# Last pair of output tiles of a two-layer streaming encoder by seven products, with the final norm in two halves of 320 tokens

## The chip, the cores and the metric

The kernel runs on one core of one Trainium2 chip. The metric is device time in microseconds (us) of one execution; lower is better. Engines are named as in the profile: PE (TensorE, matmuls) and PEld (its weight loads), DVE (VectorE), ACT (ScalarE), POOL (GpSimd) and SP (SyncE, which here only issues transfers). L12 is line 12 of the kernel before.

## What is computed

Two layers of a streaming encoder on 640 tokens (512 of a prompt, 8 x 16 of samples) with 2048 features. Each layer normalises its input, projects it with `w_in`, runs a convolution group, a window attention and a memory attention, and ends with one output projection and a residual. A last RMS norm follows the second layer:

```python
def rms_norm(x, g):
    y = x * rsqrt(mean(x * x, axis=-1, keepdims=True) + EPS)
    return y * g
...
y = concatenate([y_a, y_b, y_c], axis=-1) @ w_out      # (640, 2048) @ (2048, 2048)
x = x + y                                              # end of each layer
...
y_prompt, y_sample = rms_norm(hp, final_norm_g), rms_norm(hs, final_norm_g)
```

The mean of the last norm goes over all 2048 features of a token, so no token can be normalised before all its features are there.

## The kernel before, in words

Activations lie transposed: features on the 128 partitions, tokens along the free axis. `R` holds 16 row tiles (k = 0 to 15) of 128 features x 640 tokens in fp32. For a product each operand is split in a rounded part and a rest (`split`, L137: ACT rounds, L138, DVE subtracts, L139), and three matmuls (high x high, high x low, low x high) stand for one fp32 product. `HL` holds both parts of the 16 input tiles; `TA` and `TB` are tokens 0 to 319 and 320 to 639.

The output projection makes row tile j from 16 input tiles. Tiles 0 and 1 are done directly (`proj`, PE line L760). Tiles 2 to 15 are done in pairs (j1, j2) by `s_pair`: on 12 of the 16 input tiles (`KA`, `KB`) a 2 x 2 block scheme of Strassen's kind takes seven products of 18 matmuls for eight, on sums and differences of the weights (`sr`, made by DVE, L789 and L843) and of the inputs (`T[1]` to `T[4]`, tiles `th`, `tl`); the other four input tiles (`KS`, `rest`) are multiplied directly. All matmuls of `s_pair` are on L821 (`s_mm`): those into PSUM tiles `a` are the products on combined inputs (`mixed`) and the first product, those into `z` are `plain` and `rest`. A pair is 174 matmuls of 320 columns. The split weights (`sh`, `sl`) have two buffers each, so a split waits until PE has used up the one before the last. `add_to` (L827) adds each product to `R` on DVE. After a pair, `add_sq` squares each finished tile on ACT (L254, into `w`) and adds it into `acc` on DVE (L255).

`combos` builds `T` once per layer while PE works on tile 1: DVE subtracts in `R` in place (L789), then ACT and DVE split the differences.

In layer 1 the loop ends after tile 13; the last two tiles (14, 15) are multiplied directly (L1145, tokens 0 to 383 first, then 384 to 639). They need the upper half of inputs `KA`, which `combos` overwrites: it is saved to `y12d` in DRAM ahead of `combos` by a POOL transfer and read back in `turn`, which also replaces the buffers of `T` by buffers for the eight weight tiles (`xr`, `xh`, `xl`); for that the pair (12, 13) runs in another order (`early`: products on `T` first).

The norm: squares are summed over partitions by fp32 matmuls with a vector of ones (`tok_cols`, L222), `rsqrt` (L187 to L198) takes 12 small DVE steps, `tok_rows` (L212) spreads the result along tokens by fp32 matmuls with the identity. Then DVE multiplies each row tile by the feature factor and the row in one operation (L1178), and SP and ACT store two row tiles at a time (L1183). This is done for tokens 0 to 383 while the other tokens are multiplied, and after that for these.

All engines run their queue in order. The order in each queue is set when the program is built, by a planner that sees priorities (`tc.high_priority`) and explicit bounds (`tc.issue_after`).

Of the kernel before, what the change touches and what calls it, by code (L numbers as in the profile page):

```python
# [9 lines left out]
F32 = mybir.dt.float32  # L10
# [6 lines left out]
P = 128  # L17
D = 2048
# [40 lines left out]
def build(nc, tc, ctx, A):  # L59
# [69 lines left out]
    y12d = dr.tile([P, 6, HT], F32, tag="y12d", name="y12d")  # L129
# [87 lines left out]

    def tok_cols(srcs, inv, n=5):
        psc = pa()
        for t in range(n):  # L220
            for i, a in enumerate(srcs):
                m = pe.matmul(  # L222
                    psc[:, t:t + 1], a[:, t * P:(t + 1) * P], ones, start=i == 0, stop=i == len(srcs) - 1
                )
        cols = sml([P, n])
        col_rstd(cols, psc, n, inv)
        return cols, m.ins
# [678 lines left out]
    for l in range(L):  # L906
# [166 lines left out]
        if l == L - 1:  # L1073
            gp.dma_start(y12d, R[:, KA, TB])
# [3 lines left out]
        T, W = None, []  # L1078

        def t_prep(src):  # L1080
            with tc.high_priority():
                raw = tl([P, 512], "xr", 2, F32, cur["tw"])
                load(raw, src)
                hi = tl([P, 512], "xh", 8, F32R, cur["tw"])
                lo = tl([P, 512], "xl", 8, F32R, cur["tw"])
                split(raw, None, hi, lo)
                return hi, lo

        def turn(step):
            if step == 0:  # L1090
                close_pool("tt")
                open_pool("tw" if l == L - 1 else "wp", "right")
            if l < L - 1:
                return
            if step == 0:
                cur["y12"] = tl([P, 6, HT], "y12", 1, F32, cur["tw"])
                with tc.high_priority():
                    gp.dma_start(cur["y12"], y12d)
                return
            for p in (range(2), range(2, 8))[step - 1]:  # L1100
                W.append(t_prep(A["w_out"][l, NK - 2 + p // 4][:, p % 4 * 512:(p % 4 + 1) * 512]))
            if step == 1:
                b12 = hl(KA, TB)
                for g in (0, 3):
                    ks = slice(g, g + 3)
                    split(cur["y12"][:, ks, :], None, b12[0][:, ks, :], b12[1][:, ks, :])

        for j in list(range(2)) + list(range(2, done, 2)):
# [7 lines left out]
            else:  # L1116
                s_pair(l, j, T, resid, turn if j + 2 == done else None)
# [14 lines left out]
    ntok = [cs.stop - cs.start for cs in parts]
    sums, cols, rows, at = [None] * 2, [None] * 2, [None] * 2, []

    def in_order(f, *a):
        with tc.issue_after(at[0]) if at else nullcontext():
            r, m = f(*a)
        at[:] = [m]
        return r

    def products(ps, cs, j, k):
        wh, wl = W[j * 4 + k // 4]
        ws = slice(k % 4 * P, (k % 4 + 1) * P)
        for n, (w, lo) in enumerate(((wh, 0), (wh, 1), (wl, 0))):
            m = pe.matmul(  # L1145
                ps, w[:, ws], HL[:, lo * NK + k, cs], start=k == 0 and n == 0, stop=k == NK - 1 and n == 2
            )
        return None, m.ins

    def col_step(i):  # L1150
        cols[i] = in_order(tok_cols, [acc[:, parts[i]], sums[i]], 1.0 / D, ntok[i] // P)

    def row_step(i):
        rows[i] = in_order(tok_rows, cols[i], ntok[i] // P)[0][:, :ntok[i]]

    for i, cs in enumerate(parts):
        for j in range(2):
            ps = pz()[:, 0, :ntok[i]]
            for k in range(NK):
                if i == 1 and j == 0 and k == 5:  # L1160
                    col_step(0)
                if i == 1 and j == 0 and k == 14:
                    row_step(0)
                in_order(products, ps, cs, j, k)
            o = R[:, NK - 2 + j, cs]
            evac = ve.tensor_tensor(out=o, in0=ps, in1=res[j][:, cs], op=ALU.add)
            if j == 0:
                evac0 = evac
            sums[i] = w25()[:, cs]
            ac.activation(sums[i], o, AF.Square)  # L1170
            if j == 0:
                added = ve.tensor_tensor(out=acc[:, cs], in0=acc[:, cs], in1=sums[i], op=ALU.add)
    col_step(1)
    row_step(1)
    for i, cs in enumerate(parts):
        for k in range(NK):
# [123 lines left out]
```

## Time and profile before

| | us |
|---|---|
| median of 3 runs | 1834.02 (1833.66 to 1834.88) |
| the profiled execution, its own time | 1833.57 |
| its span in the profile | 1831.8 |
| last matmul of the last tile, add that uses it (L1166) | 1815.44 |
| first multiplication after the last `rsqrt` (L1178) | 1819.59 |

Times in the trace count from the start of the span. The span has 1.77 us less than the execution's own time. The granted clock of PE over the span is 0.996 of full speed.

### The profile page before, as it was taken

The numbers are of one execution on the slowest core, as the hardware profiler recorded it, in microseconds if no ns is written. First come the engines' busy times: TensorE is split into PE (matmuls) and PEld (weight loads), VectorE is DVE, ScalarE is ACT, GpSimd is POOL, SyncE is SP. The second block draws the span as 40 slices with busy tenths as digits, with TensorE's granted clock in tenths as the row PEclk, the third lists the DMA queues.
The fourth block names the chain that finished last, engine by engine and source line by source line (L and its number), as shares of the span: only waits on it lengthen the run. The fifth ranks groups of instructions, "written<-read, shape, count | busy, mean of one in ns | idle before, by whom it ended". The sixth has DMA issues, their size and how long they took to land.

```text
span 1831.8 us, 32312 instructions
## 1 busy us (share of the span) xinstructions
PE 1803.6 (98%) x12580; PEld 1766.5 (96%) x12580; DVE 1258.1 (69%) x2562; ACT 785.0 (43%) x1593; POOL 174.0 (9%) x383
## 2 busy tenths in 40 slices
PE   8999999999999999999999999999999999999996
PEld 7899999999999999999999999999999999989996
DVE  7959999567555445966686999766655544776765
ACT  7831224556644334533352222555755333533331
POOL 1121210000001010100030010000001110010000
PEclk9999999999999999999999999999999999999998
DMA  8844442222222343533333332222222244442233
GB/s 283 290 129 103 105 130 76 70 64 70 87 78 84 98 162 116 171 134 116 109 102 89 82 81 78 78 67 73 73 84 85 74 139 132 158 160 84 71 113 121
DMA packets 89193, 202.30 MB, mean 110 GB/s; under 512 B 12064, under 2 KB 17104, under 8 KB 89008
## 3 DMA queue, kind: packets, MB, share of 16 engines
q1 hardware_dynamic: 68848, 139.75, 25.3%
q0 software_dynamic: 17728, 57.60, 10.3%
q10 hardware_dynamic: 2464, 2.88, 0.5%
q8 instruction: 99, 1.62, 0.4%
q14 instruction: 54, 0.44, 0.1%
HBM read 184.84 MB, written 20.33 MB: 112 GB/s over the span
## 4 chain that ended last, share of the span: by engine, by line
PE 94%; DVE 3%; DMA 2%; issue 1%; ACT 0%; SPq 0%; DVEq 0%; ACTq 0%; POOLq 0%
PE z L760 59%; PE a L821 9%; PE z L821 9%; PE a L278 2%; PE z L301 2%; PE a L497 2%; PE a L540 2%; PE a L477 2%; PE z L1145 1%; DVE R L1178 1%; PE a L528 1%; DMA wr<-w_in 1%; PE a L647 1%; PE a L673 1%; PE a L686 1%
## 5 line engine op out<-in xcount | busy, mean ns | idle before, releaser
L760 PE MATMUL z<-HL,wh 128*128 128x320 f32 x4992 | 979.5, 312 | 0.0
L760 PEld LDWEIGHTS z<-HL,wh 128*128 128x128 f32 x4992 | 788.9, 188 | 7.9 <-issue 5.3
L760 PE MATMUL z<-HL,wl 128*128 128x320 f32 x2496 | 580.4, 311 | 0.7 <-DVE wl L139 0.7
L760 PEld LDWEIGHTS z<-HL,wl 128*128 128x128 f32 x2496 | 419.3, 188 | 2.0 <-DVE wl L139 1.0
L138 ACT ACTIVATE wh<-wr 128x512 fp32r<-128x512 f32 x316 | 198.7, 629 | 448.6 <-PE z L760 373.1
L139 DVE TENSOR_TENSOR wl<-wr,wh 128x512 fp32r<-128x512 f32 x316 | 218.0, 690 | 172.7 <-ACT wh L138 163.6
L425 DVE SCALAR_TENSOR_TENSOR R<-R,sm 128x128 f32<-128x128 f32 (+1 forms) x480 | 235.4, 552 | 0.1
L138 ACT ACTIVATE sh<-sr 128x768 fp32r<-128x768 f32 (+1 forms) x125 | 98.3, 787 | 206.2 <-PE a L821 91.4
L821 PE MATMUL z<-HL,sh 128*128 128x320 f32 x728 | 160.9, 309 | 1.9 <-ACT sh L138 1.9
L139 DVE TENSOR_TENSOR sl<-sr,sh 128x768 fp32r<-128x768 f32 (+1 forms) x125 | 110.1, 881 | 40.7 <-ACT sh L138 40.5
L821 PEld LDWEIGHTS z<-HL,sh 128*128 128x128 f32 x728 | 121.7, 188 | 2.4 <-ACT sh L138 2.4
L821 PE MATMUL z<-HL,sl 128*128 128x320 f32 x364 | 113.4, 312 | 0.9 <-DVE sl L139 0.7
L139 DVE TENSOR_TENSOR g<-a,g 128x512 fp32r<-128x512 f32 x80 | 49.5, 634 | 39.8 <-ACT g L138 39.2
L821 PE MATMUL a<-th,sh 128*128 128x320 f32 x234 | 72.2, 308 | 0.0
L821 PE MATMUL a<-tl,sh 128*128 128x320 f32 x234 | 72.2, 308 | 0.0
L821 PE MATMUL a<-th,sl 128*128 128x320 f32 x234 | 72.2, 308 | 0.0
L821 PEld LDWEIGHTS z<-HL,sl 128*128 128x128 f32 x364 | 68.3, 188 | 3.2 <-DVE sl L139 3.2
L821 PE MATMUL a<-HL,sh 128*128 128x320 f32 x312 | 68.9, 308 | 0.0
L138 ACT ACTIVATE g<-a 128x512 fp32r<-128x512 f32 x80 | 42.1, 551 | 53.1 <-PE a L531 29.9
L501 DVE CUSTOM_DVE_ANT_0 g<-a,R 128x256 f32<-128x256 f32 (+1 forms) x128 | 46.4, 388 | 23.4 <-PE a L497 20.0
L513 ACT ACTIVATE g<-g,sml 128x256 f32<-128x256 f32 (+1 forms) x128 | 59.8, 468 | 0.0
L485 POOL DMA_DIRECT2D R<-brep x32 | 17.3, 541 | 407.3 <-issue 238.2
(263 smaller groups left out, 2536.0 us busy)
## 6 DMA issues: line engine op xcount, KB each, us to landing
wr<-w_in SPq DMA_DIRECT2D x304, 256.0 KB, 2.7
sr<-w_out SPq DMA_DIRECT2D x52, 384.0 KB, 3.3
sr<-w_out SPq DMA_DIRECT2D x34, 256.0 KB, 2.6
u<-w_mv SPq DMA_DIRECT2D x16, 512.0 KB, 4.0
u<-cmkT POOLq DMA_DIRECT2D x16, 512.0 KB, 3.6
u<-cmv POOLq DMA_DIRECT2D x16, 512.0 KB, 4.3
u<-w_mk SPq DMA_DIRECT2D x14, 512.0 KB, 5.1
R<-xT SPq DMA_DIRECT2D x16, 320.0 KB, 4.7
```

The costliest lines, as they stand in the source:

```text
L138: a = ac.activation(hi, raw, AF.Copy)
L139: v = ve.tensor_tensor(out=lo, in0=raw, in1=hi.bitcast(F32), op=ALU.subtract)
L278: pe.matmul(ps[ct][:, :256], w[:, ws], mslot(l, k, lo), start=k == 0 and n == 0, stop=k == NK - 1 and n == 2,)
L301: pe.matmul(psv[:, m, :], mslot(l, k, lo)[:, ms], w, start=k == 0 and n == 0, stop=k == NK - 1 and n == 2,)
L425: ve.scalar_tensor_tensor(out=o, in0=x, scalar=w, in1=o, op0=ALU.mult, op1=ALU.add)
L477: pe.matmul(ps[:, :HT], w[:, ws], x[:, k, :], start=n == 0, stop=n == 11)
L497: pe.matmul(ps[:, j, c0:256], q[:, p * P:(p + 1) * P], kk[n][h][:, (p - 1) * P + c0:(p + 1) * P], start=n == 0, stop=n == 1,)
L501: ve.tensor_tensor_reduce(out=x[:, j, c0:], in0=ps[:, j, c0:], in1=bt[:, c0:], scale=1.0, scalar=-3.0e38, op0=ALU.add, op1=ALU.max, accum_ ...
L513: ac.activation(x, x, AF.Exp, bias=ng[:, p:p + 1], accum_out=sm_[:, p:p + 1])
L540: pe.matmul(po[:, os], V[h][:, v, :], p[:, ms], start=v == 0 and n == 0, stop=v == 3 and n == 1, skip_group_check=True,)
L760: pe.matmul(ps[:, s, :HT], w[:, ws], HL[:, lo * NK + k, s * HT:(s + 1) * HT], start=k == 0 and n == 0, stop=k == NK - 1 and n == 2,)
L821: pe.matmul(out, a[:, k * P:(k + 1) * P], b[:, k, :], start=start and k == 0 and i == 0, stop=stop and k == n - 1 and i == 2, skip_group_c ...
```

## The change

The last pair (14, 15) goes through the seven products too. Written out in the order of the new code, with the new kernel's names: first product `a11` into `X`, then `a21` (T[3]) into `Dd`, `s2` (T[2]) into `X`, `a22` (T[4]) into `Dd`, then `a12` on `KB`, `TA`; the direct part for `TA` (both tiles); the direct part for `TB`; then `s1` (T[1]) into `X`, and last `a12 - s2` on `KB`, `TB` in two pieces (2 and 4 input tiles). Tokens `TA` are complete before `TB`. `y12d`, the `early` order of pair (12, 13) in layer 1 and the buffers `xr`, `xh`, `xl` are gone. The feature factor is applied by ACT, in place, once per row tile (`AF.Copy` with a scale, new line L1102 for 640 tokens, L1122 for the halves of the last two tiles), and DVE multiplies 2, 3 or 4 row tiles by the row in one operation (new L1176). Sums over features use 64 tokens a matmul, five matmuls a half, each for `acc` and the last squares (new L221 and L211). Of the lower half two row tiles are multiplied before the last product ends, three after the add that takes it, and the rest after the second `rsqrt`. New lines carry numbers one lower than before up to L1066.

```diff
-        if l == L - 1:
-            gp.dma_start(y12d, R[:, KA, TB])
...
         for j in list(range(2)) + list(range(2, done, 2)):
...
-                s_pair(l, j, T, resid, turn if j + 2 == done else None)
+                s_pair(l, j, T, resid, turn if l == 0 and j + 2 == done else None)
...
                 add_sq(i, i == 0, acc)
+                if l == L - 1:
+                    ac.activation(R[:, i, :], R[:, i, :], AF.Copy, scale=sm[:, SM_FG + i:SM_FG + i + 1])
...
-    parts = (slice(0, 384), slice(384, TOK))
+    parts = (TA, TB)
...
+    def final(j, i, first):
+        cs = parts[i]
+        sq = w25()[:, cs]
+        ac.activation(sq, R[:, j, cs], AF.Square)
+        ac.activation(R[:, j, cs], R[:, j, cs], AF.Copy, scale=sm[:, SM_FG + j:SM_FG + j + 1])
+        if first:
+            return ve.tensor_tensor(out=acc[:, cs], in0=acc[:, cs], in1=sq, op=ALU.add).ins
+        sums[i] = sq
+    def cols_of(i):
+        return tok_cols([acc[:, parts[i]], sums[i]], 1.0 / D, 5, 64)
...
+    s_mm(z1[:, 1, :HT], st[0], hl(KS, TB), True, False)
+    w5 = urgent(s1)
+    s_mm(z2[:, 1, :HT], st[1], hl(KS, TB), True, True)
+    add_to(R[:, j2, TB], z2[:, 1, :HT])
+    w3 = urgent(a12)
+    s_mm(X, w5, T[1], False, True)
+    cols, m = cols_of(0)
+    def norm(i, k, n, wait=None):
+        o = R[:, k:k + n, parts[i]]
+        with tc.issue_after(wait) if wait else nullcontext():
+            ve.tensor_tensor(out=o, in0=o, in1=rows[i].unsqueeze(1).to_broadcast([P, n, HT]), op=ALU.mult)
+        return o
+    def store(k, n, cs, q):
+        q.dma_start(A["yT"][k:k + n, :, cs].rearrange("k p n -> p k n"), R[:, k:k + n, cs])
+    x3 = hl(KB, TB)
+    s_mm(z1[:, 1, :HT], [t[:, :2 * P] for t in w3], [t[:, :2, :] for t in x3], False, False)
+    m = rows_of(0, cols)
+    norm(0, 0, 2)
+    store(0, 2, TA, sy)
+    for j in (j2, j1):
+        add_to(R[:, j, TB], X)
+    added = final(j2, 1, True)
+    with tc.issue_after(m):
+        s_mm(z1[:, 1, :HT], [t[:, 2 * P:] for t in w3], [t[:, 2:, :] for t in x3], False, True)
+    evac = ve.tensor_tensor(out=R[:, j1, TB], in0=z1[:, 1, :HT], in1=R[:, j1, TB], op=ALU.add).ins
+    final(j1, 1, False)
+    norm(0, 2, 3, evac)
+    store(2, 3, TA, ac)
+    cols, m = cols_of(1)
+    with tc.issue_after(m):
+        rows_of(1, cols)
+    for n, (i, k, w) in enumerate(
+        ((0, 5, 3), (0, 8, 4), (0, 12, 4), (1, 0, 2), (1, 2, 3), (1, 5, 3), (1, 8, 4), (1, 12, 2), (1, 14, 2))
+    ):
+        norm(i, k, w, last["rsqrt"])
+        store(k, w, parts[i], ac if n % 2 else sy)
```

How the change moves instructions. Up to `combos` of layer 1 the order is the same on every engine but for the transfer to `y12d`. **First place:** DVE in layer 1 from the last gate product (L1061, new L1060) through `combos`. `R<-R` 128x3x320 are the in-place differences, `tl<-R,th` the rests of `T`, L1115 (new L1089) the add of tile 0. Before:

```order
L1061 TENSOR_TENSOR R<-R,zt_17804 128x640
L139 TENSOR_TENSOR HL<-R,HL 128x640
L789 TENSOR_TENSOR R<-R 128x3x320 x4
L1115 TENSOR_TENSOR R<-z_17849,zt_17847 128x640
L789 TENSOR_TENSOR R<-R 128x3x320
L139 TENSOR_TENSOR tl_2726_18103<-R,th_2725_18102 128x960
L789 TENSOR_TENSOR R<-R 128x3x320
```

Now:

```order
L788 TENSOR_TENSOR R<-R 128x3x320
L1060 TENSOR_TENSOR R<-R,zt_17803 128x640
L788 TENSOR_TENSOR R<-R 128x3x320
L138 TENSOR_TENSOR HL<-R,HL 128x640
L788 TENSOR_TENSOR R<-R 128x3x320 x4
L1089 TENSOR_TENSOR R<-z_17847,zt_17845 128x640
L788 TENSOR_TENSOR R<-R 128x3x320
L138 TENSOR_TENSOR tl_2726_18102<-R,th_2725_18101 128x960 x2
```

Two of the differences moved ahead; from here to the second split of tile 1's weights and beyond, the rows are those that DVE has in layer 0, in the kernel before and now, form by form.

**Second place:** ACT between two pairs of layer 1; `sh<-sr` are weight splits, `w<-R` the squares of the two finished tiles, the last `sh` of each piece is the split of `a12 - s2`. Before:

```order
L138 ACTIVATE sh_18670<-sr_18639 128x768
L254 ACTIVATE w_2792_18623<-R 128x640
L254 ACTIVATE w_2793_18626<-R 128x640
L138 ACTIVATE sh_18693<-sr_18639 128x768
L138 ACTIVATE sh_18717<-sr_18715 128x512
```

Now:

```order
L137 ACTIVATE sh_18924<-sr_18893 128x768
L253 ACTIVATE w_2824_18875<-R 128x640
L1102 ACTIVATE R<-R,sm 128x640
L253 ACTIVATE w_2825_18879<-R 128x640
L1102 ACTIVATE R<-R,sm 128x640
L137 ACTIVATE sh_18947<-sr_18893 128x768
L137 ACTIVATE sh_18971<-sr_18969 128x512
```

Each square is now followed by the scaling of its tile, so two more operations stand ahead of the split.

**Third place:** DVE at the end, around the add that takes the last product (L1166, new L1192). Before:

```order
L1166 TENSOR_TENSOR R<-z_19788,zt_19679 128x256
L1178 SCALAR_TENSOR_TENSOR R<-R,sm,a_19853 128x384 x2
L1172 TENSOR_TENSOR w_2693_17846<-w_2693_17846,w_2960_19864 128x256
L1178 SCALAR_TENSOR_TENSOR R<-R,sm,a_19853 128x384 x8
L1166 TENSOR_TENSOR R<-z_19867,zt_19680 128x256
L1178 SCALAR_TENSOR_TENSOR R<-R,sm,a_19853 128x384 x3
L187 TENSOR_SCALAR sml_19925<-a_19919 128x2
```

Now:

```order
L826 TENSOR_TENSOR R<-a_19635,R 128x320 x2
L195 SCALAR_TENSOR_TENSOR sml_19876<-sml_19875,sml_19874 64x5
L196 TENSOR_TENSOR sml_19876<-sml_19876,sml_19874 64x5
L1124 TENSOR_TENSOR w_2693_17844<-w_2693_17844,w_2959_19905 128x320
L197 SCALAR_TENSOR_TENSOR sml_19874<-sml_19876,sml_19874 64x5
L1176 TENSOR_TENSOR R<-R,a_19895 128x2x320
L1192 TENSOR_TENSOR R<-z_19637,R 128x320
L1176 TENSOR_TENSOR R<-R,a_19895 128x3x320
L186 TENSOR_SCALAR sml_19939<-a_19927 64x5
```

The first `rsqrt` (64x5) now has its last three steps behind the adds of product `s1`; 13 of 16 row tiles of the first part stood ahead of the second `rsqrt`, and now 5 do. Behind the second `rsqrt` stand 27 row tiles of 320 tokens in nine operations (3, 4, 4, then 2, 3, 3, 4, 2, 2), where 3 of 384 and 16 of 256 tokens stood.

## Rows read from the trace of the kernel before

**Rows 1.** The page: busy time, share of the span and instructions of each engine, and the chain that ended last, by engine.

```profile
PE 1803.6 (98%) x12580; PEld 1766.5 (96%) x12580; DVE 1258.1 (69%) x2562; ACT 785.0 (43%) x1593; POOL 174.0 (9%) x383
...
PE 94%; DVE 3%; DMA 2%; issue 1%; ACT 0%; SPq 0%; DVEq 0%; ACTq 0%; POOLq 0%
```

**Rows 2.** The chain of waits of the last 130 us in order of time (start us, us, what, count): pairs of layer 1, then the last two tiles.

```profile
1723.03 13.20 PE a L821 x90
1736.24 12.50 PE z L821 x84
1748.73 23.76 PE a L821 x162
1772.49 9.68 PE z L821 x66
...
1803.56 1.23 PE a L222 x12
...
1808.11 0.67 PE a L212 x6
```

**Rows 3.** The timeline of the end (start us, us, engine, line, operation, out<-in, shape, count, idle before it and what ended it), DVE, ACT, PE and SP.

```profile
1815.44 0.42 DVE L1166 TENSOR_TENSOR R<-z,zt 128x256 f32<-128x256 f32 x1
...
1815.95 0.42 ACT L1170 ACTIVATE w<-R 128x256 f32<-128x256 f32 x1 [5.50 <-DVE R L1166]
...
1816.42 0.83 PE L222 MATMUL a<-ones,w 128*128 128x1 f32 x6 [1.20 <-ACT w L1170]
...
1817.35 0.16 DVE L187 TENSOR_SCALAR sml<-a 128x2 f32<-128x2 f32 x1
...
1819.59 7.93 DVE L1178 SCALAR_TENSOR_TENSOR R<-R,sm,a 128x384 f32<-128x384 f32 x19
...
1820.22 0.37 SPq L1183 DMA_DIRECT2D yT<-R  x1
```

**Rows 4.** Stretches of the end: their length, busy time of the engines (instructions), granted clock of PE, mean busy share of the 16 DMA engines, GB/s. In the first stretch stores of 384 tokens run, in the other two stores of 256.

```profile
1814.50:1817.50 3.00, 1.55 (x14) 1.38 (x12) 3.00 (x7) 0.42 (x1) 0.00 (x0) 1.00 1.01 365
...
1824.50:1829.00 4.50, 0.00 (x0) 0.00 (x0) 3.01 (x8) 0.00 (x0) 0.00 (x0) 0.50 1.01 343
1827.60:1829.00 1.40, 0.00 (x0) 0.00 (x0) 0.00 (x0) 0.00 (x0) 0.00 (x0) 0.50 1.00 343
```

**Rows 5.** PE's timeline where it waits behind `combos`, in layer 0 (first row) and in layer 1.

```profile
767.61 0.57 PE L760 MATMUL z<-HL,sl 128*128 128x320 f32 x2 [1.35 <-DVE sl L139]
...
1621.31 0.56 PE L760 MATMUL z<-HL,sl 128*128 128x320 f32 x2 [2.33 <-DVE sl L139]
...
1631.26 0.41 PE L821 MATMUL z<-HL,sl 128*128 128x320 f32 x1 [0.30 <-DVE sl L139]
1635.29 0.56 PE L821 MATMUL z<-HL,sh 128*128 128x320 f32 x2 [1.41 <-ACT sh L138]
1636.28 0.42 PE L821 MATMUL z<-HL,sl 128*128 128x320 f32 x1 [0.43 <-DVE sl L139]
```

**Rows 6.** The chain of waits in layer 0 and in layer 1 at the first `mixed` products (start us, us, what, count).

```profile
789.72 13.20 PE a L821 x90
...
1645.93 13.20 PE a L821 x90
```

**Rows 7.** Who waited for whom on DVE in layer 1's output projection (engine line, waited for: us in total, times, longest).

```profile
DVE R L789 <- DMA y12d<-R: 3.0, 1, 3.0
```

**Rows 8.** The timeline of ACT, DVE and PEld between two pairs of layer 1, one of five alike (columns as in rows 3).

```profile
1708.86 0.74 ACT L254 ACTIVATE w<-R 128x640 f32<-128x640 f32 x1 [0.23 <-DVE R L827]
1710.49 0.74 ACT L254 ACTIVATE w<-R 128x640 f32<-128x640 f32 x1 [0.89 <-DVE w L255]
1711.42 0.84 ACT L138 ACTIVATE sh<-sr 128x768 fp32r<-128x768 f32 x1 [0.19 <-DVE sr L789]
...
1712.38 0.95 DVE L139 TENSOR_TENSOR sl<-sr,sh 128x768 fp32r<-128x768 f32 x1
...
1713.38 0.19 PEld L821 LDWEIGHTS z<-HL,sl 128*128 128x128 f32 x1 [0.17 <-DVE sl L139]
```

**Rows 9.** The groups of instructions by line and form: a scaling on ACT of 640 tokens with a factor for each partition (line, form, count | busy us, mean ns | idle before).

```profile
L141 ACT ACTIVATE HL<-R,sm 128x640 fp32r<-128x640 f32 x32 | 25.3, 822 | 5.7 <-PE z L821 5.1 <-PE z L301 0.5
```

**Rows 10.** The timeline of DVE: two operations of 960 columns in a row, and two of 320 (columns as in rows 3).

```profile
1617.36 2.22 DVE L139 TENSOR_TENSOR tl<-R,th 128x960 fp32r<-128x960 f32 x2
...
1707.94 0.89 DVE L827 TENSOR_TENSOR R<-a,R 128x320 f32<-128x320 f32 x2 [0.42 <-PE a L821]
```

**Rows 11.** The chain of waits in layer 1's memory attention: 16 instructions, which are 8 fp32 matmuls, on stationary operands of 32 columns.

```profile
1586.35 0.59 PE a L715 x16
```

More of the change, by code (lines that the diff above doesn't have):

```diff
@@ L222, in tok_cols @@
                 m = pe.matmul(
-                    psc[:, t:t + 1], a[:, t * P:(t + 1) * P], ones, start=i == 0, stop=i == len(srcs) - 1
+                    psc[:, t:t + 1], a[:, t * w:(t + 1) * w], ones, start=i == 0, stop=i == len(srcs) - 1
                 )
-        cols = sml([P, n])
+        cols = sml([w, n])
         col_rstd(cols, psc, n, inv)
@@ L1077, in build @@
         done = NK if l == 0 else NK - 2
[L1078 to L1087, printed above, removed]
+        T = None
         def turn(step):
@@ L1091, in turn @@
                 close_pool("tt")
[L1092 to L1106, printed above, removed]
+                open_pool("wp", "right")
         for j in list(range(2)) + list(range(2, done, 2)):
@@ L1126, in build @@
                 add_sq(i, i == 0, acc)
-    res = [zt(), zt()]
-    for j in range(2):
-        gp.dma_start(res[j], x1d[NK - 2 + j])
-    parts = (slice(0, 384), slice(384, TOK))
[L1132 to L1176, printed above, removed]
-            with tc.issue_after(last["rsqrt"] if k >= 13 else (evac if k >= 10 else added if k >= 2 else evac0).ins):
-                ve.scalar_tensor_tensor(
-                    out=R[:, k, cs], in0=R[:, k, cs], scalar=sm[:, SM_FG + k:SM_FG + k + 1], in1=rows[i],
-                    op0=ALU.mult, op1=ALU.mult,
-                )
-            if k % 2:
-                (sy if k % 4 == 1 else ac).dma_start(
-                    A["yT"][k - 1:k + 1, :, cs].rearrange("k p n -> p k n"), R[:, k - 1:k + 1, cs]
-                )
@@ L1186, in build @@
-    close_pool("tw")
+                if l == L - 1:
+                    ac.activation(R[:, i, :], R[:, i, :], AF.Copy, scale=sm[:, SM_FG + i:SM_FG + i + 1])
+    j1, j2 = NK - 2, NK - 1
+    wj = [A["w_out"][L - 1, j1], A["w_out"][L - 1, j2]]
+    cut = [slice(ks.start * P, ks.stop * P) for ks in (KA, KB, KS)]
+    for j in (j1, j2):
+        gp.dma_start(R[:, j, :], x1d[j])
+    X, Dd = pa()[:, :HT], pa()[:, :HT]
+    z1, z2 = pz(), pz()
+    parts = (TA, TB)
+    sums, rows = [None] * 2, [None] * 2
@@ new lines, in urgent @@
+    def urgent(src):
+        with tc.high_priority():
+            return s_split(src)
+    def final(j, i, first):
[8 more added lines that the diff above has]
+        return tok_cols([acc[:, parts[i]], sums[i]], 1.0 / D, 5, 64)
@@ new lines, in rows_of @@
+    def rows_of(i, cols):
+        ps = pa()
+        m = col_row([ps], cols, 5, 64)
+        rows[i] = ps[:, :HT]
+        return m
+    with tc.high_priority():
+        a11 = s_load(wj[0][:, cut[0]])
+        a21 = s_load(wj[1][:, cut[0]])
+        a22 = s_load(wj[1][:, cut[1]])
+        a12 = s_load(wj[0][:, cut[1]])
+        p1 = s_split(a11)
+        s1, s2 = s_raw(), s_raw()
+        ve.tensor_tensor(out=s1, in0=a21, in1=a22, op=ALU.add)
+        sub(s2, s1, a11)
+        sub(a21, a11, a21)
@@ new lines, in build @@
+    s_mm(X, p1, hl(KA, TA), True, True)
+    add_to(R[:, j1, TA], X)
+    s_mm(Dd, urgent(a21), T[3], True, True)
+    add_to(R[:, j2, TB], Dd)
+    s_mm(X, urgent(s2), T[2], False, True)
+    add_to(R[:, j2, TA], X)
+    s_mm(Dd, urgent(a22), T[4], False, True)
+    add_to(R[:, j2, TA], Dd)
+    s_mm(z1[:, 0, :HT], urgent(a12), hl(KB, TA), True, False)
+    with tc.high_priority():
+        st = [s_load(w[:, cut[2]]) for w in wj]
+        sub(a12, a12, s2)
+    st = [urgent(t) for t in st]
+    s_mm(z1[:, 0, :HT], st[0], hl(KS, TA), False, True)
```

19 lines of the change are left out of this document (12 added, 7 removed).

## The prediction, as put on record before the run

> **What bounds the kernel now.** The page comes first: PE is busy for 98% of the span and makes 94% of the chain that ended last, DVE 3% and DMA 2% [rows 1]. So two things can move the end: how long PE is held before the last product, and what runs after it. The chain in order of time shows the pairs of layer 1 following each other without a gap: one is 13.20 + 12.50 = 25.70 us [rows 2]. The timeline shows the end. The add of the last product starts at 1815.44, the second `rsqrt` at 1817.35, the first multiplication behind it at 1819.59, and the span ends at 1831.8 [rows 3]. These last 12.21 us have two candidates for a limit. DVE works 7.93 us [rows 3], and the 16 DMA engines are fully busy (share 1.00 to 1.02) at 343 to 365 GB/s while it does; at 343 also from 1827.60 to 1829.00, when no engine computes any more [rows 4]. So the stores end last and DVE just keeps up with them. The reader should see that the tail is a matter of bytes not yet stored when the second `rsqrt` ends.
>
> The sum goes against the profiled execution, 1833.57 us (span 1831.8 and 1.77 around it); the median of the runs is 0.45 above it. A difference of about 0.2%, 3.7 us, is what a measurement of this kernel can tell from no change.
>
> **The change part by part.**
>
> *Layer 1 up to the first products on T.* The transfer to `y12d` goes, and with it 3.0 us in which DVE waits inside `combos` [rows 7]; behind it PE waits 2.33 + 0.30 + 1.41 + 0.43 us [rows 5]. DVE now runs in the order of layer 0, so layer 0 is the price list. From the matmul that PE is first held at (start less wait [rows 5]) to the first `mixed` product [rows 6] it takes 789.72 - 766.26 = 23.46 us in layer 0 and 1645.93 - 1618.98 = 26.95 in layer 1: 3.5 us less. Two scalings of 0.82 us [rows 9] are new on ACT in this stretch, one ahead of the split for which PE waits last; I give back 0.5. **-3.0 us**, between -1.5 (only the first wait shrinks) and -3.5 (layer 0 exactly). The eight loads and splits of plain weights and the read back of `y12d` go too; PE didn't wait for these. On SP's queue six loads take the place of the eight and come in the rhythm of every pair; on POOL's queue the two loads of the last residuals wait for nothing that is late, since their place in `R` is free after `combos`.
>
> *The scalings between pairs.* In the pairs (4,5) to (12,13) two scalings stand ahead of the split of `a12 - s2`. The first falls in ACT's wait of 0.89 us [rows 8] and costs nothing. The second starts when the second square ends, at 1711.23, or up to 0.1 earlier (operations in a row overlap by about that, on DVE too [rows 10]), and takes 0.82; so the split starts at 1711.85 to 1712.05 instead of 1711.42, and the rest `sl` on DVE 0.88 after it, at 1712.73 to 1712.93 instead of 1712.38: 0.35 to 0.55 late. There is no cover: PE's weight load already waits 0.17 us for this `sl` [rows 8]. Five times 0.45 is **+2.2 us**, 1.75 to 2.75 at the ends. DVE gets rid of nothing here, so this is the cost of moving the factor to ACT.
>
> *The last pair.* Pair (12,13) ends at 1772.49 + 12.50 = 1784.99 in any order, and the last add comes 30.45 us later now. In its place stand one pair, 25.70, and in the stream ten fp32 sums and five spreading matmuls. A spreading matmul is 0.67 / 3 = 0.22 us [rows 2], five are 1.1. A sum on 128 columns is 1.23 / 6 = 0.205 us [rows 2]; on 64 columns no row shows it, on 32 it is 0.59 / 8 = 0.074 [rows 11]. I take 0.11, the value nearest to half of the first; ten are 1.1. There is a new wait: the last three steps of the first `rsqrt` stand on DVE behind the two adds of `s1`'s product, 2 x 0.40 [rows 10], with an `acc` add of 0.40 between them. So the spreading can start 0.05 + 0.8 + 3 x 0.2 + 0.4 = 1.85 us after that product, and PE has only 6 matmuls, 0.88 us, in between: it stands for 1.0, and the last 12 products stand behind it. Sum 25.7 + 1.1 + 1.1 + 1.0 = 28.9: **-1.5 us**. The add starts at 1815.44 - 3.0 + 2.2 - 1.5 = 1813.1.
>
> *From that add to the first multiplication behind the second rsqrt.* Now it takes 4.15 us [rows 3]: 0.51 to the square, 0.42 for it, three sums in 0.83, 0.1, and 2.24 for `rsqrt`. Then the square has 320 tokens (0.47) and nine sums follow it, 9 x 0.11 + 0.2 = 1.2 (0.83 less 3 x 0.205 is the 0.2): 4.6 us, **+0.45**, from +0.1 at 0.074 a sum to +1.3 at 0.205. DVE fills this with three row tiles. The spreading behind is hidden: DVE has 11 row tiles of the lower half first.
>
> The Trainium skill, TensorE: Matmul & The Clock Gate, LDWEIGHTS (loading the stationary operand), says that a weight load takes time by its columns, P / 1.2 ns; with two loads a sum that would be an estimate of 0.107 us for 64 columns and 0.213 for 128. The trace has 0.205 for 128 [rows 2] and nothing for 64.
>
> *The stores.* Behind the second `rsqrt` stood 4 row tiles of 384 tokens (the pair 12, 13 of the first part was only half done) and 16 of 256: 4 x 196,608 + 16 x 131,072 B = 2.88 MB. The first store was issued at 1820.22 [rows 3], 0.63 us after the first multiplication, and the span ended 11.58 later. At 346 GB/s, between the two rates of rows 4, the bytes are 8.33 us of it, so 3.25 are fixed (start and landing). Now 27 row tiles of 163,840 B are left, 4.42 MB. A run of 320 tokens lies halfway between 256 and 384, so I take 355 GB/s, halfway between 343 and 365: 12.46 us (12.1 to 12.9). The first store follows a group of three row tiles, 1.15 us + 0.03. Sum 1.18 + 3.25 + 12.46 = 16.9 instead of 12.2: **+4.7 us**. DVE can't be the limit: 960 columns take 1.07, 320 take 0.40 [rows 10], that is 0.33 a row tile and 0.07 an operation, 27 x 0.33 + 9 x 0.07 = 9.6 us. That is also why fewer and larger DVE operations buy nothing here: DVE gets faster than the stores, and what it saved earlier it doesn't use, since only 5 row tiles instead of 13 are multiplied ahead of the second `rsqrt`.
>
> Sum: -3.0 + 2.2 - 1.5 + 0.45 + 4.7 = +2.85 us. 1833.57 + 2.85 = 1836.4, and with the 0.45 of the median **1836.9 us**: a loss within what can't be told from no change. PE ends some 2 us earlier and the tail takes more than that back.
>
> **The rivals.**
>
> *The small sums cost what they cost now* (0.205 us, whatever their columns): nineteen of them lie on the path, ten in the stream and nine in the tail, 19 x 0.095 = +1.8, so 1838.7, slower by 0.26%. From 0.15 us a sum on it decides. For it: only 128-column rows exist in this form. Against: rows 11. Chance 0.19.
>
> *Layer 1 keeps its wait.* If DVE's work in `combos` and ACT's new scalings, not the transfer, hold PE, the -3.0 is lost: 1839.9, slower. For it: DVE had little idle time there beside those 3.0 us. Against: layer 0, same order, waits 1.35 us once. Chance 0.1.
>
> *The scalings hide.* If ACT's splits have more slack than rows 8 show, 2.2 us fall away: 1834.7, no change. Chance 0.13.
>
> *Larger stores run faster.* The stores grow from 262 and 393 KB to 328 to 655 KB. If it was the size that made 343 and 365, and not the run, 390 GB/s is a fair extension: 11.3 us, 1835.8, no change. Against: the share is 1.0 already. Chance 0.1. The Trainium skill, DMA: Bandwidth & Descriptors, Measured (under Bandwidth), has the rule to batch transfers to 1 MiB or more, with 341 GB/s at 1 MB and 425 at 16 MB, for loads; by 425 the bytes would be an estimate of 10.4 us. No row here goes over 365 for stores.
>
> *The end gets shorter.* If stores and DVE both kept up with the norm so that the 5 early row tiles and the larger groups made the tail no longer than now, -4.7 would be left: 1832.2, still no change; only with layer 0's full 3.5 and free scalings is it 1829.5, faster by 0.25%. Chance 0.05.
>
> **How the numbers follow.** The forecast itself has 0.43, and of that 0.04 lies over 3.7 us, where several of its terms are at their high ends. Slower: 0.19 + 0.1 + 0.04 = 0.33; faster 0.05; within 0.2% the rest, 0.62. With all low ends the sum is about +0.5 (1834.5), with the high ones, and either slower rival, +6 (1840.1). The range goes from 1834.3 to 1840.2.
>
> **What would show it.** In the profile of the changed kernel: one wait of PE of about 1.3 us at the splits of tile 1, and the first `mixed` product 3 us earlier; then PE waits of 0.4 to 0.6 us for `sl` once in each of five pairs, 26.1 us apart; PE standing about 1 us before the first spreading matmuls; the last add near 1813; nine sums in 1.2 us; DMA share 1.0 at about 355 GB/s for 12.5 us up to 2.3 us before the end. The forecast is wrong if the tail from the last add to the end is under 20 us (it would be 21.5, and is 16.4 now), if the pairs stay at 25.70, or if layer 1's waits stay.

## The result: 3.4 us slower in the median, 0.18%

The changed kernel takes 1837.74 us (median of 14 runs, 1835.15 to 1840.17), the kernel before on the same chip 1834.38 (14 runs). The ratio is 1.0018, 95% interval 1.0010 to 1.0025. So the loss can be told here, though it lies under the 0.2% that the prediction took as the least that can. 1836.9 was forecast, in a range of 1834.3 to 1840.2. The profiled execution took 1836.55 us, span 1834.7, which is 2.9 us over the span before; the forecast's sum was +2.85. One run of the experiments, of ten of the kernel with stores of one row tile, took 2524.5 us at a granted clock of 0.653, where its others have 0.993 to 0.995, and is left out of medians and ratios.

The page of the changed kernel, as [rows 1]: PE has the same work within 1 us, DVE has 4 us more, and ACT 14, the scalings. Nothing on this page tells that three terms of 2.5 to 4.5 us moved.

```profile
PE 1804.6 (98%) x12592; PEld 1766.7 (96%) x12592; DVE 1262.0 (69%) x2550; ACT 799.1 (44%) x1610; POOL 172.8 (9%) x381
```

PE's timeline behind `combos` in layer 1, as [rows 5]: one wait of 1.04 us is left of four that made 4.47. (PE's weight loads wait 0.41 us once more, at 1632.36, which this view of PE doesn't show.)

```profile
1619.91 0.56 PE L759 MATMUL z<-HL,sl 128*128 128x320 f32 x2 [1.04 <-DVE sl L138]
```

The chain of waits there (start us, us, what, count), as [rows 6] and [rows 8]. The first product on T starts at 1642.02, 3.91 us sooner than before. Then a scaling (ACT, line 1102) stands in the chain ahead of the split `sh`, and 26.20 us lie between one pair and the next (1642.02 to 1668.22), where before it was 25.70.

```profile
1642.02 10.58 PE a L820 x72
...
1655.95 0.11 ACT R L1102
...
1656.69 0.84 ACT sh L137
...
1668.22 10.57 PE a L820 x72
```

The timeline of PE and DVE at the end, as [rows 3]: the sums of the lower half between products (here one and six of its ten), the wait of 0.83 us for the first `rsqrt` and the spreading behind it, the last add at 1813.49, nine sums, the first multiplication behind the second `rsqrt` at 1817.98.

```profile
1801.96 0.28 PE L221 MATMUL a<-ones,w 128*64 128x1 f32 x2
1804.12 0.86 PE L221 MATMUL a<-ones,w 128*64 128x1 f32 x12
...
1810.16 1.32 PE L211 MATMUL a<-ident,sml 64*128 64x64 f32 x10 [0.83 <-DVE sml L197]
...
1814.54 1.21 PE L221 MATMUL a<-ones,w 128*64 128x1 f32 x18 [0.88 <-ACT w L1121]
...
1813.49 0.49 DVE L1192 TENSOR_TENSOR R<-z,R 128x320 f32<-128x320 f32 x1 [1.14 <-PE z L820]
...
1817.98 9.65 DVE L1176 TENSOR_TENSOR R<-R,a 128x960 f32<-128x960 f32 x9
```

Stretches of the end (columns as in [rows 4]): the DMA engines are full from 1820.0 to 1832.5, 12.5 us, at 350 GB/s in the mean and 352 to 359 from 1822 on, the last 4.9 us of them with DVE, PE and ACT idle (DVE ends at 1827.6). The stores end last, as forecast.

```profile
1825.00:1828.00 3.00, 0.00 (x0) 0.00 (x0) 2.64 (x3) 0.00 (x0) 0.00 (x0) 0.50 1.03 352
1828.00:1831.00 3.00, 0.00 (x0) 0.00 (x0) 0.00 (x0) 0.00 (x0) 0.00 (x0) 0.50 1.04 357
1831.00:1832.50 1.50, 0.00 (x0) 0.00 (x0) 0.00 (x0) 0.00 (x0) 0.00 (x0) 0.50 1.04 359
```

### The profile page after: what moved, and what is told of

It is laid out like the page before. It is cut to its first block, busy times and chain, and to the rows that moved or that the text cites. A ratio compares the mean times of both kernels' runs of the same rounds, so it can differ in the third digit from the quotient of the medians.

```text
span 1834.7 us, 32327 instructions
## 1 busy us (share of the span) xinstructions
PE 1804.6 (98%) x12592; PEld 1766.7 (96%) x12592; DVE 1262.0 (69%) x2550; ACT 799.1 (44%) x1610; POOL 172.8 (9%) x381
## 3 DMA queue, kind: packets, MB, share of 16 engines
q10 hardware_dynamic: 2160, 2.56, 0.4%
## 4 chain that ended last, share of the span: by engine, by line
PE 95%; DVE 2%; DMA 1%; ACT 1%; issue 1%; DVEq 0%; ACTq 0%; POOLq 0%
PE z L759 61%; PE a L820 9%; PE z L820 8%; PE a L277 3%; PE z L300 2%; PE a L496 2%; PE a L539 2%; PE a L476 2%; PE a L527 1%; DMA wr<-w_in 1%; PE a L646 1%; DVE sl L138 1%; PE a L672 1%; PE a L685 1%; PE a L530 1%
## 5 line engine op out<-in xcount | busy, mean ns | idle before, releaser
L137 ACT ACTIVATE sh<-sr 128x768 fp32r<-128x768 f32 (+1 forms) x134 | 105.6, 788 | 221.6 <-PE a L820 95.5
L820 PE MATMUL z<-HL,sh 128*128 128x320 f32 x784 | 173.4, 309 | 0.5 <-ACT sh L137 0.5
L138 DVE TENSOR_TENSOR sl<-sr,sh 128x768 fp32r<-128x768 f32 (+1 forms) x134 | 117.8, 882 | 50.6 <-ACT sh L137 50.5
L820 PEld LDWEIGHTS z<-HL,sh 128*128 128x128 f32 x784 | 131.0, 188 | 0.9 <-ACT sh L137 0.8
L820 PE MATMUL z<-HL,sl 128*128 128x320 f32 x392 | 122.2, 312 | 2.5 <-DVE sl L138 2.2
L820 PE MATMUL a<-tl,sh 128*128 128x320 f32 x252 | 77.7, 309 | 0.0
L820 PE MATMUL a<-th,sh 128*128 128x320 f32 x252 | 77.7, 308 | 0.0
L820 PE MATMUL a<-th,sl 128*128 128x320 f32 x252 | 77.7, 308 | 0.0
L820 PE MATMUL a<-HL,sh 128*128 128x320 f32 x336 | 74.3, 309 | 0.0
L826 DVE TENSOR_TENSOR R<-a,R 128x320 f32<-128x320 f32 x84 | 39.9, 489 | 25.6 <-PE a L820 25.2
```

The costliest lines, as they stand in the source:

```text
L137: a = ac.activation(hi, raw, AF.Copy)
L138: v = ve.tensor_tensor(out=lo, in0=raw, in1=hi.bitcast(F32), op=ALU.subtract)
L820: pe.matmul(out, a[:, k * P:(k + 1) * P], b[:, k, :], start=start and k == 0 and i == 0, stop=stop and k == n - 1 and i == 2, skip_group_c ...
L826: ve.tensor_tensor(out=out, in0=ps, in1=out, op=ALU.add)
```

## The experiments

Ratios are to the kernel before, run on the same chip as the experiment; one thousandth is 1.83 us. The experiments ran on several chips, so kernels are compared by these ratios. The theory is the forecast's: the transfer's hold gave time back, the scalings and the tail's stores took it.

### The transfer to `y12d`, left out

```
# in the kernel before
-        if l == L - 1:
-            gp.dma_start(y12d, R[:, KA, TB])
...
-                    gp.dma_start(cur["y12"], y12d)
+                    gp.dma_start(cur["y12"], x1d[10:16, :, HT:].rearrange("k p n -> p k n"))
```

> The kernel before without the copy of the upper tokens of row tiles 10 to 15 to device memory; the last two row tiles read other numbers back in its place (rows of the first layer's result), so that their tokens 320 to 639 are other numbers. Theory (the copy's hold): DVE waits 3.0 us for this copy before it can overwrite those row tiles, and all mixed tiles of layer 1 come that much later; without it the first mixed product starts near 1642 (1645.93 before, 1642.02 in the changed kernel), and the time falls by 3.0 to 3.9 us, to 1830.5 to 1831.4 us (0.998). Rival (the stretch is bound by DVE's own subtractions and splits, and the changed kernel gained there by having no second read-back and no splits of it to prepare): the first mixed product stays within 0.5 us of 1645.9, and the time within 0.5 us of before.

Measured: 1829.93 us, ratio 0.9978 (0.9969 to 0.9987), 4.1 us under the median of before, a little more than the 3.0 to 3.9 expected. DVE's operations in `combos` now follow each other where [rows 7] had the 3.0 us, PE's wait is again 1.04 us, and the first product on T starts at 1642.21. PE's timeline, and below it the chain:

```profile
1620.09 0.57 PE L759 MATMUL z<-HL,sl 128*128 128x320 f32 x2 [1.04 <-DVE sl L138]
```

```profile
1642.21 13.20 PE a L820 x90
...
1745.01 23.76 PE a L820 x162
...
1807.60 4.20 DVE R L1175 x8
1811.80 0.34 DVE R L1163
```

So the whole gain of the changed kernel in layer 1 comes from this one hold: without it the old code reaches the first product within 0.2 us of the new (1642.02). The rival (DVE's own work holds PE) falls. The eight weight splits that the change removes are all still in this kernel, and neither ACT nor DVE stands in its chain from 1745.0 to 1805.8, so they cost nothing here, as forecast.

### The same transfer, sent sooner

```
# in the kernel before
-            gp.dma_start(y12d, R[:, KA, TB])
+            for g in range(6):
+                gp.dma_start(y12d[:, g, :], R[:, KA.start + g, TB])
```

> The kernel before with the copy of the upper tokens of row tiles 10 to 15 issued as six copies, one a row tile, so that each can go once its row tile is final; nothing is left out. Theory (it is when the copy ends, not that there is one): DVE's wait for it shrinks from 3.0 us to that of the last row tile, under 0.5 us, and the time falls by 2.5 to 3.5 us, to 1831 to 1832 us. Rival (six copies on one queue go out one behind the other and no sooner, since all wait for the queue's turn): within 0.5 us of the 1834.4 of before.

Measured: 1829.56 us, ratio 0.9978 (0.9969 to 0.9987), with nothing left out: 4.3 us under before, more than the 2.5 to 3.5 expected, and faster than both kernels. The operations' view of `y12d`: six copies, the first issued at 1429.6 and the last at 1606.3, where one was issued at 1604.6; nobody on DVE waits for them. The last is issued no sooner than the one was, but it carries one row tile in place of six. In DVE's timeline four subtractions run in a row where the 3.0 us were. That there is a copy costs nothing; that it was one copy, behind the last row tile, was the cost. The view of operations, then DVE's timeline:

```profile
L1075 POOL DMA_DIRECT2D y12d<-R x6: 544/544/555, 1429.6 to 1606.3; - x6
```

```profile
1607.76 4.61 DVE L789 TENSOR_TENSOR R<-R 128x960 f32<-128x960 f32 x4
```

The chain at the first product on T:

```profile
1643.81 13.20 PE a L821 x90
```

The profiled execution (1831.12) reaches the first product on T 1.6 us after that of the kernel without the copy. The stretches of both at the same place show why (this kernel first): behind a wait of PE of 1.84 us, where the other has 1.04, PE's granted clock was 0.57 in the mean of 4 us (0.50 from 1622 to 1625), and 19 matmuls ran there in place of 29, at a DMA share of 0.93 and 0.94. It is one execution's; the medians of the two kernels lie within 0.4 us.

```profile
1621.40:1625.40 4.00, 4.00 (x19) 4.00 (x18) 3.48 (x5) 0.84 (x1) 1.59 (x3) 0.57 0.93 325
```

```profile
1621.40:1625.40 4.00, 4.00 (x29) 4.00 (x29) 3.96 (x6) 1.86 (x2) 1.59 (x3) 1.00 0.94 331
```

### The scalings behind the next pair's splits

```
# in the changed kernel
+    def scale_tile(i, wait):
+        with tc.issue_after(wait):
+            ac.activation(R[:, i, :], R[:, i, :], AF.Copy, scale=sm[:, SM_FG + i:SM_FG + i + 1])
...
-                    ac.activation(R[:, i, :], R[:, i, :], AF.Copy, scale=sm[:, SM_FG + i:SM_FG + i + 1])
+                    owed.append(i)
...
# in rest(), behind the split of the direct part's weights
+            if owed:
+                scale_tile(owed.pop(0), cur["split"])
```

> The changed kernel with the two scalings of a pair on ACT issued behind the next pair's split of its direct weights, one each, not ahead of them. Theory (the scalings stand ahead of the next pair's splits on ACT, and TensorE waits for these): the pairs go from 26.2 back to 25.7 us, five of them, 2.5 us, to about 1835.2 us against 1837.7 of the changed kernel. Rival (the pair's 0.5 us comes from the squares, the adds or DVE, and the scalings are hidden): pairs stay at 26.2 us and the time at 1837.7.

Measured: 1834.48 us, ratio 1.0004 (0.9995 to 1.0013), against 1.0018 of the changed kernel: 2.6 us back, 2.5 were expected. The chain has no ACT or DVE between the pairs any more, and they are 25.70 us apart. In ACT's timeline the scaling (now line 775) stands where ACT waited for PE or a load. The chain, of a pair and of the end:

```profile
1642.22 13.20 PE a L826 x90
...
1667.92 13.20 PE a L826 x90
...
1745.02 13.20 PE a L826 x90
...
1811.22 0.50 DVE R L1202
```

ACT's timeline:

```profile
1662.53 0.63 ACT L137 ACTIVATE sh<-sr 128x512 fp32r<-128x512 f32 x1 [3.22 <-DMA sr<-w_out]
1663.07 0.81 ACT L775 ACTIVATE R<-R,sm 128x640 f32<-128x640 f32 x1
```

This kernel and the one without the copy reach 1745.0 together (1745.02 and 1745.01), so their difference is the last pair and the tail alone: 4.2 us between the spans (1832.4 and 1828.2), a ratio of 1.0004 to 0.9978, 4.8 us, on the same chip. The last add comes 0.6 us sooner here (1811.22 against 1811.80), and the end 4.8 us later behind it (21.2 us against 16.4). The 0.6 is not all PE's: without the copy, that add stands behind eight multiplications that DVE does until 1811.80. So against the old kernel without the hold seven products for the last pair bring 0.6 us at most up to the last add, and the tail that came with them, with 27 row tiles of 320 tokens left behind the second `rsqrt`, costs 4.8; how much of that its order makes, the last experiments show.

### The factor back on DVE

```
# in the changed kernel; the scalings on ACT go
-            ve.tensor_tensor(out=o, in0=o, in1=rows[i].unsqueeze(1).to_broadcast([P, n, HT]), op=ALU.mult)
+        for t in range(n):
...
+            ve.scalar_tensor_tensor(out=o[:, t, :], in0=o[:, t, :],
+                scalar=sm[:, SM_FG + k + t:SM_FG + k + t + 1], in1=rows[i], op0=ALU.mult, op1=ALU.mult)
```

> The changed kernel with the feature factors back on DVE: no scalings on ACT, and in the tail one instruction with both factors for each row tile, in place of one for two to four. Theory (the scalings cost the pairs 2.5 us; the tail's end is set by the stores at 355 GB/s, which 27 single instructions of 0.4 to 0.47 us, 11 to 12.7 us, just keep up with): pairs back at 25.7 us, the tail 0 to 1 us longer, 1835.2 to 1836.2 us against 1837.7. Rival (the tail hangs on DVE, and single instructions lose there what the pairs gain): 1837 us or more.

Measured: 1835.67 us, ratio 1.0007 (0.9998 to 1.0015), 2.0 us better than the changed kernel, as expected. The pairs are 25.70 apart. In the tail DVE needs 12.45 us for 27 row tiles in place of 9.65, and the end comes 17.4 us after its first one in place of 16.7. DVE's timeline, and a stretch of the end: the stores run at 352 to 355 GB/s from 1822 to 1830 all the same.

```profile
1816.62 12.45 DVE L1174 SCALAR_TENSOR_TENSOR R<-R,sm,a 128x320 f32<-128x320 f32 x27
```

```profile
1824.00:1827.00 3.00, 0.00 (x0) 0.00 (x0) 3.00 (x8) 0.00 (x0) 0.00 (x0) 0.50 1.01 355
```

So the part of the change that made DVE's tail 2.8 us shorter (factors on ACT, rows in groups) is worth 0.7 us at the end and costs 2.5 between the pairs.

### Stores of one row tile

```
# in the changed kernel, behind the second rsqrt
-        store(k, w, parts[i], ac if n % 2 else sy)
+        for t in range(w):
+            store(k + t, 1, parts[i], ac if (k + t) % 2 else sy)
```

> The changed kernel with the same multiplications behind the second rsqrt, but each row tile sent by a store of its own (164 KB) in place of stores of two to four row tiles. Theory (the rate goes by the 1,280 bytes of a token run, not by the size of a store): the same 352 to 359 GB/s, the same end within 0.5 us, 1837.7. Rival (larger stores run faster): 27 stores of 164 KB run under 340 GB/s, and the end comes over 0.7 us later.

Measured: 1837.17 us (nine runs), ratio 1.0016 (1.0007 to 1.0026): the same as the changed kernel's 1.0018. 27 stores of 164 KB run at the rate of nine of 328 to 655 KB; from the first multiplication to the end it is 16.4 us (1821.56 to 1838.0). The rival falls at these sizes.

```profile
1825.00:1828.00 3.00, 0.00 (x0) 0.00 (x0) 3.00 (x4) 0.00 (x0) 0.00 (x0) 0.50 1.01 353
```

### Sums of 80 tokens

```
# in the changed kernel
-        return tok_cols([acc[:, parts[i]], sums[i]], 1.0 / D, 5, 64)
+        return tok_cols([acc[:, parts[i]], sums[i]], 1.0 / D, 4, 80)
```

> The changed kernel with each half's sums of squares cut into 4 pieces of 80 tokens instead of 5 of 64: 8 matmuls in place of 10 for a half, 4 that spread the result in place of 5. Theory (a sum's matmul costs by its token columns between the 0.135 to 0.144 us of 64 and the 0.205 of 128): 0.15 to 0.16 us each, 1.2 to 1.3 us a half, no change of the time that can be told. Rival (it costs a fixed 0.14 us whatever the columns): 1.1 us a half. By the time itself neither can be told.

One run: 1835.65 us. PE's timeline: 12 instructions, six sums, take 0.95 us, 0.158 a sum, in the interval expected; the changed kernel's six take 0.86, 0.143. So the rival, a fixed price, falls for sums in a row; one sum alone takes 0.24 here and 0.28 at 64 columns. One run's time settles nothing, but the profile shows more than was expected: from the start of the last pair's combined products (1773.10; 1772.99 in the changed kernel) to the last add it takes 39.55 us where the changed kernel takes 40.50, with two sums and one spreading fewer on the way and shorter stretches of products between them (12 in 1.87 us, not 1.95). The timeline, and below it the chain:

```profile
1801.98 0.24 PE L221 MATMUL a<-ones,w 128*80 128x1 f32 x2
1803.93 0.95 PE L221 MATMUL a<-ones,w 128*80 128x1 f32 x12
```

```profile
1802.22 1.87 PE z L820 x12
...
1812.65 0.50 DVE R L1192
```

### The lower half ahead of the last products

```
# in the changed kernel: cols_of(0) ahead of z2's last product, rows_of(0) three k blocks into s1's,
# the lower half multiplied and stored while the last products run
-((0, 5, 3), (0, 8, 4), (0, 12, 4), (1, 0, 2), (1, 2, 3), (1, 5, 3), (1, 8, 4), (1, 12, 2), (1, 14, 2))
+((0, 14, 2), (1, 0, 2), (1, 2, 3), (1, 5, 3), (1, 8, 4), (1, 12, 2), (1, 14, 2))
```

> The changed kernel with the sums and the rsqrt of tokens 0 to 319 ahead of the last two products, so that 14 of the 16 lower row tiles are multiplied and sent before the second rsqrt instead of 5. Theory (behind the second rsqrt the stores set the end: 27 row tiles of 164 KB at 355 GB/s are 12.5 us, 18 are 8.3): from the first multiplication behind the second rsqrt to the end 16.7 goes to about 10 us, but the second rsqrt itself comes up to 2.6 us later, since DVE does lower multiplications before it; together 3.5 to 4.5 us faster than the changed kernel, 1833.2 to 1834.2 us. Rival (TensorE waits for the first rsqrt and the lower multiplications hold the last adds and the second sums, so that what the stores gain the chain loses): within 1.5 us of 1837.7.

Measured: 1834.02 us, ratio 1.0002 (0.9993 to 1.0011), 2.9 us better than the changed kernel, under the 3.5 to 4.5 expected. The stores behind the second `rsqrt` are a third fewer, but its chain is late: DVE multiplies lower rows from 1813.34 until 1816.26, although the sums are there 1.1 us before. From the first multiplication behind the second `rsqrt` (1818.46) to the end it is 13.8 us, not about 10: only one multiplication stands over the spreading, and the next starts at 1821.08. The next experiments look at this. DVE's and PE's rows:

```profile
1813.34 3.01 DVE L1177 TENSOR_TENSOR R<-R,a 128x640 f32<-128x640 f32 x4
...
1813.98 1.21 PE L221 MATMUL a<-ones,w 128*64 128x1 f32 x18 [0.62 <-ACT w L1121]
```

### Both edits

> The changed kernel with both edits: the late scalings and the early lower half. Theory (two places, each on the path by itself, so they add): 6.0 to 7.0 us faster than the changed kernel, 1830.7 to 1831.7 us, and so 2.7 to 3.7 us faster than the kernel before. Rival (the late scalings only let TensorE run into the tail's stores and the first rsqrt sooner, which then wait): no better than the early lower half alone by over 1 us.

Measured: 1831.52 us, ratio 0.9986 (0.9977 to 0.9995): 5.9 us better than the changed kernel, where the two edits alone gave 2.6 and 2.9, 5.5 together, and 6.0 to 7.0 were expected. They add. It is faster than the kernel before, by 2.5 us. DVE and PE at its end: the four multiplications ahead of the second `rsqrt` last until 1812.9, over 1 us after the nine sums; the spreading behind it takes 2.37 us in place of 1.32, at a granted clock of 0.50 where it was 1.00, behind 3.49 us in which PE has stood, and one multiplication of 0.81 covers it.

```profile
1809.95 3.01 DVE L1187 TENSOR_TENSOR R<-R,a 128x640 f32<-128x640 f32 x4
...
1817.69 5.81 DVE L1187 TENSOR_TENSOR R<-R,a 128x640 f32<-128x640 f32 x6 [1.82 <-PE a L211]
...
1810.58 1.21 PE L221 MATMUL a<-ones,w 128*64 128x1 f32 x18 [0.63 <-ACT w L1129]
1815.29 2.37 PE L211 MATMUL a<-ident,sml 64*128 64x64 f32 x10 [3.49 <-DVE sml L197]
```

### Both edits, the spreading covered

```
# in the kernel with both edits
-    for k, q in ((6, sy), (8, sy), (10, sy), (12, ac)):
+    for k, q in ((6, sy), (8, ac)):
...
-((0, 14, 2), (1, 0, 2), ...
+((0, 10, 2), (0, 12, 2), (0, 14, 2), (1, 0, 2), ...
```

> The kernel with both edits, but six lower row tiles (10 to 15) multiplied behind the second rsqrt, where it had two. Theory (with both edits DVE's lower multiplications hold the second rsqrt 1.1 us after the sums are there, and the spread behind it takes 2.4 us at half the clock with 0.8 us of work over it; two row-tile pairs moved there give both back): the first multiplication of the upper half starts about 1.1 us sooner, 0.5 to 1 us faster than the kernel with both edits, 1830.5 to 1831 us. Rival (the stores set the end whatever DVE does: 22 row tiles of 164 KB, 10.2 us, behind the second rsqrt in place of 18, 8.3 us): no gain, or up to 0.7 us slower, 1831.5 to 1832.2 us.

Measured: 1829.78 us, ratio 0.9979 (0.9970 to 0.9988), against 0.9986 of the one above (on another chip): 1.3 us by the ratios, over the 0.5 to 1 expected, with intervals that overlap. DVE's timeline: the first multiplication of the upper half starts 1.47 us sooner, of which 0.44 was there before the tail (the sums of its lower half start at 1798.46 in the chain, the other's at 1798.90), so 1.03 us is the edit's. DVE waits for the spreading 0.35 us in place of 1.82.

```profile
1813.60 2.27 DVE L1187 TENSOR_TENSOR R<-R,a 128x640 f32<-128x640 f32 x3
1816.22 5.81 DVE L1187 TENSOR_TENSOR R<-R,a 128x640 f32<-128x640 f32 x6 [0.35 <-PE a L211]
```

So the kernel with seven products for the last pair can be brought 7.1 us under the changed kernel (0.9979 against 1.0018) and 3.9 under the kernel before; but the kernel before with its copy sent sooner is as fast (0.9978). A gain of the seven products over that is not shown.

## Why the prediction was right

The time came out 0.84 us over the forecast, 0.1 of it in the profiled execution. That the sum of this came so near (+2.85 and +2.9) is luck: layer 1 gave 0.9 us more than was said, and the last pair 0.95 less. The terms in the profile of the changed kernel stand to it as follows.

| step of the forecast | said | measured |
|---|---|---|
| layer 1 up to the first product on T | -3.0 | -3.9 |
| the scalings between five pairs | +2.2 | +2.5 (5 x 0.50) |
| the last pair up to the last add | -1.5 | -0.55 |
| the add to the multiplication behind the second `rsqrt` | +0.45 | +0.34 (4.49) |
| from there to the end | +4.7 | +4.5 (16.72) |
| sum | +2.85 | +2.9 |

**Layer 1: the mechanism was right, the size was not.** The forecast gave back 0.5 us for two scalings ahead of the split that PE waits for last; the first two row tiles' scalings held nothing. The new stretch, 1642.02 less the start of its first wait (1619.91 - 1.04), is 23.15 us, 0.3 below layer 0, so even the end of the range (-3.5) was too small. The two kernels around `y12d` show that it is the hold; without the copy 0.2 us of the gain are left over.

**The scalings: right in place and nearly in size.** ACT's squares and scalings follow each other without a gap from 1653.55 to 1656.69, and the pair is longer by 0.50, in the interval of 0.35 to 0.55.

**The last pair: 0.95 us of the 1.5 failed to come.** The chain, from the direct part to the last product (start us, us, what, count):

```profile
1794.11 7.92 PE z L820 x54
1802.03 0.21 PE a L221 x2
1802.24 1.95 PE z L820 x12
1804.19 0.79 PE a L221 x12
1804.98 0.49 PE a L820 x2
1805.47 0.44 PE a L221 x6
1805.91 2.56 PE a L820 x16
...
1810.16 1.32 PE a L211 x10
1811.49 1.98 PE z L820 x12
```

Two prices were low: the ten sums took 1.44 us, not 1.1, and the spreading 1.32, not 1.1. Two were high: the wait for the first `rsqrt` was 0.83, not 1.0, and the pair itself. The 25.70 us of a pair hold 0.18 that the last one doesn't have: 174 products at 0.147 us are 25.52, and 84 on `z` take 12.50 [rows 2] with the weight load's wait [rows 8], while these 54 run through in 7.92. And a term was missing: each of the four stretches of products behind fp32 operations takes about 0.2 us over its number at 0.147 (12 in 1.95 and 1.98 for 1.76, 2 in 0.49 for 0.29, 16 in 2.56 for 2.35), 0.8 in all. Together these are 0.34 + 0.22 - 0.17 - 0.18 + 0.8 = 1.0 us, which is what is missing. Whether the 0.2 is the price of the change from fp32 operations to products is not shown: two of the stretches end in an add on DVE that waits for the last product.

PE's timeline tells more of the sums' price. One sum takes 0.28, 0.24 and 0.28 us at 64, 80 and 128 columns, and six take 0.86, 0.95 and 1.40; so each further sum of a block takes 0.116, 0.142 and 0.224, in proportion to the columns. The 0.11 of the forecast was nearly right for that, and the nine sums in the tail took the 1.2 us said. What it left out in the stream is what each of three blocks costs besides. At 128 columns, in the kernel before:

```profile
1803.40 1.40 PE L222 MATMUL a<-ones,w 128*128 128x1 f32 x12
...
1814.95 0.28 PE L222 MATMUL a<-ones,w 128*128 128x1 f32 x2
```

The Trainium skill, TensorE: Matmul & The Clock Gate, LDWEIGHTS (loading the stationary operand), whose rule gave an estimate of 0.107 us for a sum at 64 columns and 0.213 at 128, agrees with the trace for a further sum of a block (0.116 and 0.224); the first sum of a block costs more.

**The tail: right.** 355 GB/s was taken from the length of a token's run, and 350 in the mean and 352 to 359 from 1822 on were measured; the store's size changed nothing. The add to the end took 21.2 us, where 21.5 was said, and the DMA engines were full for 12.5 us until 2.2 us before the end, where 2.3 was said. The rival of larger stores fell with the stores of one row tile. By the rule of the Trainium skill, DMA: Bandwidth & Descriptors, Measured (under Bandwidth), to batch transfers to 1 MiB or more, the larger stores should have been the faster ones. The runs don't show it at these sizes: 353 GB/s with stores of 164 KB, 352 to 359 with stores of 328 to 655 KB.

**The other rivals.** That the small sums cost 0.205 whatever their columns: no; six take 0.86 us, 0.143 each, which is nearer to the forecast's 0.11. That layer 1 keeps its wait: no. That the scalings hide: no, until they are issued behind the next pair's splits. That the end gets no longer: no, by 4.5 us.

The median lies 3.4 us over before, the profiled executions 2.9 apart: the changed kernel's median is 1.19 over its profiled execution, where the forecast took the 0.45 of the kernel before. The falls of PE's clock told in the last section fit this, a term that the forecast lacked; they were not isolated.

## What to carry to other kernels

A change of several parts that comes out at nearly nothing may be a gain of 4 us and two losses: run each part alone before it is kept or dropped; here the gain needed one place of the old kernel, and the rest of the change, as it stood, was against it. A copy that protects data from being overwritten should leave in pieces, each when its own rows are final. Work that is moved to a less busy engine is still in the queue of that engine: ask what stands behind it, and issue it behind that.

## What the runs showed of the hardware

PE's granted clock fell to 0.50, its level of 1.2 GHz, for some us in three of the profiled executions, at two places, and each time it cost 1.5 to 1.8 us: behind `combos` in the kernel with six copies, and in the tail of the kernels with the factor on DVE and with stores of one row tile. The last one (1839.9 us, 2.7 over its own median) shows it: behind the same wait of 0.83 us and the same ten spreading operations as in the changed kernel, the clock goes to 0.50 by 1814, the products there take 2.93 us and not 1.98, and the nine sums behind them 2.08 and not 1.21. With the factor on DVE these products take 3.44 us. The changed kernel's stretch of the same work kept 1.00, and fell only when PE had stood from 1815.8 on. The rows of that execution, PE's timeline, and a stretch:

```profile
1811.91 1.32 PE L211 MATMUL a<-ident,sml 64*128 64x64 f32 x10 [0.83 <-DVE sml L197]
...
1817.24 2.08 PE L221 MATMUL a<-ones,w 128*64 128x1 f32 x18 [0.78 <-ACT w L1121]
```

```profile
1814.00:1815.00 1.00, 1.00 (x6) 1.00 (x5) 0.10 (x1) 0.00 (x0) 0.00 (x0) 0.50 0.00 0
```

Every run's mean granted clock is on record. Of the changed kernel and the three with the same order on PE in the tail (late scalings, the factor on DVE, stores of one row tile) 21 of 45 runs have 0.993 or 0.994; of the three kernels with the lower half ahead none of 33, and of the kernel before 3 of 75. In the changed kernel these are six of 14 runs, median 1839.0 us, and the other eight have 1837.3. So the order of the tail seems to bring such a fall in about half of its executions. A mean doesn't say where the clock fell, and what decides whether it falls was not tried.

PE's weight loads of 64 columns for the sums start together with their matmuls, behind 0.19 us of idling (1804.12 in the changed kernel); those of 80 columns start 0.14 us ahead of theirs (1803.79 and 1803.93), those of 128 columns, in the kernel before, 0.12 (1803.28 and 1803.40). This stands beside the shorter stretches of products at 80 columns; that it is their cause was not tried.
